# Attention scores of a streaming-encoder layer: the product with the low part of k on 64 rows per map, the two maps in different halves of the array

## The chip, the cores and the metric

One NeuronCore of one Trainium2 chip runs the whole layer as one program. The metric is the time of the program on the device in microseconds (us), as the median of several runs. The profile is one profiled execution on the chip. Its engines are PE (TensorE matmuls), PEld (TensorE weight loads), DVE (VectorE), ACT (ScalarE), POOL (GpSimd) and SP (the queue that issues most DMAs). In a matmul row of a view, `128*96` means 128 rows of the array by 96 columns, and what follows is the shape of the moving operand.

## What is computed

The layer works on 1024 tokens of width 1024: a joint projection, a gated linear recurrence (RG-LRU), differential attention, a cross-attention to 256 memory tokens and a mixture of 32 experts. The change is in the differential attention. It has 8 heads, each with two maps (`m`) of head dimension 64, and a chunk-causal mask:

```python
def diff_attention(q, k, v, ...):
    q = q.reshape(bsz, s, ATTN_HEADS, 2, ATTN_HEAD_DIM)
    k = k.reshape(bsz, s, ATTN_HEADS, 2, ATTN_HEAD_DIM)
    ...
    for blk in range(s // Q_BLOCK):
        q0, q1 = blk * Q_BLOCK, (blk + 1) * Q_BLOCK
        sc = jnp.einsum('bqhmd,bkhmd->bhmqk', q[:, q0:q1], k[:, :q1]).astype(jnp.float32)
        mask = (jnp.arange(q1) // CHUNK)[None, :] <= (jnp.arange(q0, q1) // CHUNK)[:, None]
        p = jax.nn.softmax(jnp.where(mask, sc, NEG_INF), axis=-1)
        w = p[:, :, 0] - lam * p[:, :, 1]
        outs.append(jnp.einsum('bhqk,bkhd->bqhd', w.astype(v.dtype), v[:, :q1]))
```

Everything is float32. The kernel gets its precision by splitting each operand x of a product into two parts, x = high + low, that the array takes as `float32r`.

## The kernel before

**Stages.** q, k and v of all heads are projected first and kept in DRAM. Then comes the attention, head by head, with projections of the gates (`pga`) and of two LRU channels fed in between as filler. After it come the LRU, the merge, the memory attention, the routing and the experts, whose 32 steps stream their weights from DRAM.

**Loading a head.** `head_load(h)` loads q and k of each map twice, to partitions 0 to 63 and to 64 to 127, and splits them. `qS` (per map) has the high part of q in its upper half (partitions 0 to 63) and the low part in its lower half. `kH` (per map) has the high part of k in both halves, and `kL` (per map) has the low part of k in both halves. The tiles come from one pool of 51 slots of 128 x 1024.

**Scores.** `scores(h, qb)` takes a query block of 128 and the nk = qb + 1 key blocks before it. For each map and each piece of keys (`CUTS`: one piece of 256, 384 or 512 keys up to nk = 4, two pieces above) it issues two products into the same PSUM bank: `qS` with `kH` (L474), which gives (high + low) of q times high of k, and `qS` with `kL` (L475), which gives (high + low) of q times low of k. Both use all 128 rows of the array. Up to nk = 4 the two maps lie in two banks of one PSUM tile `pS`; above, each map has a PSUM tile of its own, of two banks. DVE masks (L478, L481) and takes the maximum (L479, L482), ACT takes the exponential (L486). `combine` joins the two maps on POOL and DVE (L495, L496), `w_transpose` turns the result on PE (`pw`, L516) and splits it into `wT` (L519, L520), and `pv` multiplies with v (`po`, lines L152 to L154 of the helper `mm3`).

**Order.** The loop at the end of `filler` calls scores, filler, combine, transposes and products in turn, with the amounts of filler in the table `FV`. A scheduler then settles the order of each engine by a simulated timeline. PE executes its instructions in that order.

Of the kernel before, what the change touches and what calls it, by code (L numbers as in the profile page):

```python
# [20 lines left out]
T = 1024          # tokens  # L21
D = 1024          # model width
P = 128
NB = T // P       # token blocks
NH = 8            # attention heads
NE = 32           # experts
MT = 256          # memory tokens
CAP = 96          # tokens of a block of an expert
# [5 lines left out]
# columns of the packed per-channel vectors  # L34
C_NMIX, C_NMEM = 0, 8
C_CW = 16         # 4 x 8
# [3 lines left out]
# offsets in the packed row vector  # L40
# [4 lines left out]
class Weights:  # L45
    """Streams [128, 1024] float32 weight pieces and splits each exactly into two float32r parts.

    Loads run `load_ahead` pieces before the splits, splits `split_ahead` pieces before their use;
    order-only edges keep the scheduler from running further ahead and taking the slots."""
# [49 lines left out]
    def prefetch(self, n):  # L99
        """Loads up to n pieces ahead of the splits, from the last matmul so far on."""  # L100
        self.floor, self.load_ahead = self.last, n
        self.load()
# [22 lines left out]
def block_kernel(ctx, tc, a):  # L125
# [30 lines left out]
    # ---------------------------------------------------------------- weights  # L156
# [9 lines left out]
    EARLY = [1, 4]      # LRU channels projected beside the attention  # L166
# [26 lines left out]
    # ------------------------------------------------- first loads, constants  # L193
# [23 lines left out]
    def rstd_of(ss, n, cnt, name):  # L217
        """(ss / cnt + eps) ** -0.5 on [128, n]."""
        t = sm.tile([P, 16], F32, tag="rs0", name=name + "m")
        r = sm.tile([P, 16], F32, tag="rs1", name=name + "r")  # L220
        G.tensor_scalar(t[:, :n], ss, 1.0 / cnt, EPS, op0=OP.mult, op1=OP.add)
        G.tensor_tensor(r[:, :n], t[:, :n], negh[:, :n], op=OP.pow)
        return r
# [12 lines left out]
    def transposed(srcs, gain, dst_h, dst_l, name, nk=8):  # L236
        """srcs: token-major tiles; writes [channel, 128 * len(srcs)] per k, scaled by gain[:, k]."""
        n = len(srcs) * P
        for k in range(nk):
            ps = bank(f"{name}p{k}")  # L240
            for j, s in enumerate(srcs):
                E.transpose(ps[:, j * P:(j + 1) * P], s[:, k * P:(k + 1) * P], ident)
            h, l = dst_h(k), dst_l(k)
            A.activation(h, ps[:, :n], AF.Copy, scale=gain[:, k:k + 1])
            V.scalar_tensor_tensor(l, ps[:, :n], gain[:, k:k + 1], f(h), op0=OP.mult, op1=OP.subtract)

    # ------------------------------------------------------ RMSNorm(x), h1^T
# [13 lines left out]
    # -------------------------------------- rotary tables, lambda, q/k gains  # L261
# [52 lines left out]
    # ------------------------- q, k, v: normalised, rotated, kept in DRAM  # L314
    # per head: q, k as [2 maps x 64] x tokens; per head pair: v token-major
# [7 lines left out]
    def tm_proj(w, half, name):  # L323
        """[128 tokens, 4, 256]: the 512 tokens of a half, token-major."""
        ps = bank2(name, F32, (P, 4, 256))
        for j in range(4):
            c = slice((4 * half + j) * P, (4 * half + j) * P + P)
            for k in range(8):
                wh, wl = (x[:, (k % 4) * 256:(k % 4) * 256 + 256] for x in w[k // 4])
                mm3(ps[:, j, :], hH[k][:, c], hL[k][:, c], wh, wl, k == 0, k == 7)  # L330
            if j % 2 == 1:
                W.tick()
            if j == 1:
                yield 5.2
        return ps
# [58 lines left out]
    # ------------------------- merge gates (2 sigmoid - 1 = tanh(x / 2)), in DRAM  # L394
    tg_d = dp.tile([16, P, T], F32, name="tg_d")

    def cm_unit(w, xh, xl, ps_halves):
        """[128 output channels, 1024 tokens], channel-major."""
        wh, wl = w
        for half in range(2):  # L400
            c = slice(half * 512, half * 512 + 512)
            for k in range(8):
                kc = slice(k * P, k * P + P)
                mm3(ps_halves[half], wh[:, kc], wl[:, kc], xh[k][:, c], xl[k][:, c], k == 0, k == 7)
# [22 lines left out]
    # --------------------------------------------------- differential attention  # L427
# [3 lines left out]
    def head_load(h):  # L431
        """Per map: q stacks its two parts on the partitions, k repeats each part."""
# [9 lines left out]
        yield  # L442
        for m in range(2):
            kh_[h, m], kl_[h, m], qs[h, m] = (slot(f"{x}{h}_{m}", F32R) for x in ("kH", "kL", "qS"))
            split(raw.pop((1, m)), kh_[h, m], kl_[h, m])
            yield
            t = raw.pop((0, m))
            A.activation(qs[h, m], t, AF.Copy)
            V.tensor_tensor(qs[h, m][64:128, :], t[64:128, :], f(qs[h, m][64:128, :]), op=OP.subtract)
            del t  # L450
            yield
# [8 lines left out]
    def scores(h, qb):  # L460
# [6 lines left out]
        both = bank2(f"pS{h}_{qb}", F32, (P, 2, 512)) if nk <= 4 else None  # L467
        for m in range(2):
# [3 lines left out]
            lhs = qs[h, m][:, qb * P:(qb + 1) * P]  # L472
            for c in CUTS[nk]:
                E.matmul(ps[:, o:o + c], lhs, kh_[h, m][:, o:o + c], start=True, stop=False)  # L474
                E.matmul(ps[:, o:o + c], lhs, kl_[h, m][:, o:o + c], start=False, stop=True)  # L475
                o += c
            if nk > 4:
                V.memset(ps[0:64, n - 64:n], NEG)  # L478
                V.reduce_max(mx[:, m:m + 1], ps[:, :n], axis=AX.X, negate=True)  # L479
            elif m == 1:  # L480
                V.memset(both[0:64, :, n - 64:n], NEG)  # L481
                V.tensor_reduce(mx, both[:, :, :n], axis=AX.X, op=OP.max, negate=True)  # L482
# [16 lines left out]
    def w_transpose(h, g):  # L499
        """Transposes of the query pair g; parts per two key blocks: [128 keys, 2, 256 queries]."""  # L500
# [121 lines left out]
    for h in range(NH):  # L622
# [12 lines left out]
        for m in range(2):  # L635
            del qs[h, m], kh_[h, m], kl_[h, m]
# [5 lines left out]
    # ------------------------------------------------------------------ RG-LRU  # L642
# [5 lines left out]
    V.tensor_tensor(t1, t0, lam, op=OP.min)                      # -|lam|  # L648
    V.tensor_scalar(t0, t0, 0.0, None, op0=OP.max)
    G.tensor_tensor(t2_, ebase[:, 0:8], t1, op=OP.pow)           # y = exp(-|lam|)  # L650
    V.tensor_scalar(t3, t2_, 2.0, None, op0=OP.add)
    V.reciprocal(t3, t3)
    V.tensor_tensor(t3, t3, t2_, op=OP.mult)                     # z = y / (2 + y)
# [6 lines left out]
    V.scalar_tensor_tensor(t5, t5, 2.0, t0, op0=OP.mult, op1=OP.add)   # softplus(-lam)  # L660
# [48 lines left out]
    def lru_gate(c):  # L709
        """2 * gelu of the gate."""  # L710
# [12 lines left out]
    def lru_scan(c):  # L723
        """Block-diagonal gates, recurrence, times the gate."""
# [25 lines left out]
    # memory keys and values  # L750
# [87 lines left out]
    # --------------------------------- attention output, gated: 2 * sigmoid(g) * y  # L838
# [12 lines left out]
    # -------------------------------------------------- LRU output, merge, w_out  # L851
# [22 lines left out]
    # ------------------------------------------- memory attention, MoE input  # L874
# [20 lines left out]
    def pair_T(src, kp, name):  # L895
        """Channels 256 * kp ... of two token blocks: parts [128 channels, 2 parts, 2, 256 tokens]."""
# [128 lines left out]
    def st_R(tb):  # L1025
        """Transposes of a token block for the router: parts [128 channels, 4, 256 tokens]."""
# [12 lines left out]
    def st_L(g):  # L1039
        """Router logits of two token blocks: [36 high and 36 low parts, 256 tokens]."""  # L1040
# [17 lines left out]
    # ----------------------------------------------------------------- routing  # L1058
    rpool = {}

    def rt(name, *shape, dt=F32):
        """Routing tiles, cut out of slots."""
# [34 lines left out]
    def st_route(b0, n2):  # L1097
        """Choices of n2 token blocks, then their ranks within the experts and dispatch codes."""
# [14 lines left out]
        def first_hot(v, mxv, n):  # L1113
            """One-hot of the first maximum along the last axis."""
# [37 lines left out]
        # weights of the two choices  # L1152
# [12 lines left out]
        # per expert and slot: row code, weight in two parts  # L1165
# [90 lines left out]
    def b3(ap, n):      # [P, NB] -> [P, NB, n]  # L1256
# [11 lines left out]
    def table(code, parts, w_, ix):  # L1268
        """[slots, n]: token - 2 T (0: none), weight parts -> weights, rows (out of bounds: none)."""
# [7 lines left out]
    # ----------------------------------------------------------------- experts  # L1277
# [68 lines left out]
    def more_blocks():  # L1346
        """Blocks beyond the first per expert: count, first and end in the list of such blocks."""
# [42 lines left out]
    # further blocks of experts with more than CAP tokens  # L1390
# [4 lines left out]
    with tc.For_i(0, n_more, 1):  # L1395
# [9 lines left out]
        V.tensor_scalar(eb[:, 2:3], eb[:, 2:3], float(CAP), None, op0=OP.mult)      # -CAP * block of the expert  # L1405
# [40 lines left out]
def _layout(i):  # L1446
# [4 lines left out]
    def cm(m):      # [1024, n * 128] -> [n, 128, 8 * 128]  # L1451
# [3 lines left out]
    def tm(m, c):   # [K, n * c] -> [n, pieces, 128, 1024]  # L1455
# [4 lines left out]
    def col(v):     # [n * 128] -> [128, n]  # L1460
        return v.reshape(-1, 128).T
# [41 lines left out]
```

## Time and profile before

| what | us |
|---|---|
| median of 3 runs | 1963.01 (1957.44 to 1965.14) |
| span of the profiled execution | 1957.1 |
| what lies around the span in the profiled execution | not listed apart; the lowest of the three runs is 0.3 above the span |
| first to last start of a score product (L474, L475) | 328.7 to 720.0 |
| products with `kL` (L475) | 192: 96 of 512 keys, 64 of 256, 32 of 384 |

A view has one row for each group of instructions: line, engine, operation, tiles, shapes, count, busy time and the mean duration of one in ns, and the idle time before it. In a timeline a row has the start, the duration, the instruction, and in brackets how long its engine had been idle and what ended that. Matmuls are pipelined: the next one starts before the record of the last one ends. What a matmul takes of PE is therefore read from start to start.

### The profile page before, as it was taken

To read this page: it belongs to the slowest core of one execution; us is meant where nothing else is said; L and a number is where in the kernel's file an instruction comes from. 1 tells how busy PE (TensorE), PEld (TensorE's weight loads), DVE (VectorE), ACT (ScalarE), POOL (GpSimd) and SP (SyncE) were. 2 spreads that over 40 slices of the span, in tenths; PEclk is the share of its full clock that TensorE was granted. 3 is DMA by queue.
4 is the path that set the end of the run, shared out by engine and by line. 5 is a ranking of instruction groups with operands and counts; after the bars stand their busy time and mean duration, and the time that the engine had idled before them with its cause. 6 is when DMAs were issued, how large, how long until landed. Compare 5 with 4: busy or idle time off the path is not lost. (4 is left out here: it accounts for less than half of the span.)

```text
span 1957.1 us, 27981 instructions
## 1 busy us (share of the span) xinstructions
PE 1882.8 (96%) x10366; PEld 1551.2 (79%) x10366; DVE 1295.3 (66%) x1766; ACT 1087.6 (56%) x1607; POOL 337.1 (17%) x430
## 2 busy tenths in 40 slices
PE   7999999999999999989999999996999999999996
PEld 7999998888888888867888888885777777777664
DVE  5222233777778767887534434776899999999985
ACT  5222223555555545875412214543788888888885
POOL 2343251122222221110000000211111111111110
PEclk9999999999999999989999999998999999999998
DMA  4222225433334322214422511167999999999996
GB/s 167 98 80 94 87 87 152 133 99 115 96 108 120 107 81 79 82 51 173 150 67 84 197 33 65 54 248 296 297 340 361 345 349 360 340 354 342 352 368 217
DMA packets 103130, 353.53 MB, mean 181 GB/s; under 512 B 14224, under 2 KB 15376, under 8 KB 102992
## 3 DMA queue, kind: packets, MB, share of 16 engines
q1 hardware_dynamic: 91088, 322.10, 46.7%
q0 software_dynamic: 7296, 17.04, 3.8%
q10 hardware_dynamic: 4608, 12.58, 1.6%
q8 instruction: 82, 1.34, 0.3%
q14 instruction: 56, 0.46, 0.1%
HBM read 311.82 MB, written 48.23 MB: 184 GB/s over the span
## 5 line engine op out<-in xcount | busy, mean ns | idle before, releaser
L94 DVE TENSOR_TENSOR wl<-wraw,wh 128x1024 fp32r<-128x1024 f32 x480 | 578.4, 1230 | 104.2 <-ACT wh L90 91.9
L90 ACT ACTIVATE wh<-wraw 128x1024 fp32r<-128x1024 f32 x480 | 496.4, 1057 | 111.3 <-DVE wl L94 18.3
L153 PE MATMUL pgu<-wl,xeh 128*96 128x512 f32 x512 | 203.5, 397 | 1.2 <-DVE wl L94 1.0
L152 PE MATMUL pgu<-wh,xeh 128*96 128x512 f32 x512 | 203.4, 397 | 0.3 <-ACT wh L90 0.3
L154 PE MATMUL pgu<-wh,xel 128*96 128x512 f32 x512 | 200.9, 392 | 0.0
L486 ACT ACTIVATE p<-pS,st 128x256 f32<-128x256 f32 (+7 forms) x128 | 94.9, 747 | 93.7 <-DVE st L479 53.2
L154 PE MATMUL pqk<-wh,hL 128*128 128x256 f32 x512 | 145.2, 284 | 0.0
L153 PE MATMUL pqk<-wl,hH 128*128 128x256 f32 x512 | 145.1, 283 | 0.0
L152 PE MATMUL pqk<-wh,hH 128*128 128x256 f32 x512 | 145.0, 283 | 0.0
L152 PE MATMUL pga<-hH,wh 128*128 128x512 f32 x320 | 127.8, 399 | 3.5 <-DVE wT L520 3.5
L153 PE MATMUL pga<-hL,wh 128*128 128x512 f32 x320 | 126.3, 395 | 0.0
L154 PE MATMUL pga<-hH,wl 128*128 128x512 f32 x320 | 125.9, 393 | 0.0
L153 PEld LDWEIGHTS pgu<-wl,xeh 128*96 128x96 f32 x512 | 82.8, 162 | 44.0 <-DVE wl L94 13.0
L152 PEld LDWEIGHTS pgu<-wh,xeh 128*96 128x96 f32 x512 | 82.8, 162 | 33.8 <-ACT wh L90 0.5
L154 PEld LDWEIGHTS pgu<-wh,xel 128*96 128x96 f32 x512 | 82.8, 162 | 33.1 <-DVE xel L321 0.2
L1332 POOL DMA_INDIRECT out<-y,idx x32 | 46.5, 1453 | 357.2 <-ACT y L1331 352.6
L495 POOL TENSOR_SCALAR p<-p,st 128x128 f32<-128x128 f32 (+3 forms) x64 | 55.9, 873 | 294.4 <-DVE st L494 203.4
L153 PE MATMUL py<-wl,ah 128*96 128x512 f32 x256 | 101.8, 398 | 0.5 <-DVE wl L94 0.5
L154 PE MATMUL py<-wh,ah 128*96 128x512 f32 x256 | 100.5, 392 | 0.0
L152 PEld LDWEIGHTS pqk<-wh,hH 128*128 128x128 f32 x512 | 98.2, 192 | 0.0
L153 PEld LDWEIGHTS pqk<-wl,hH 128*128 128x128 f32 x512 | 98.2, 192 | 0.0
L154 PEld LDWEIGHTS pqk<-wh,hL 128*128 128x128 f32 x512 | 98.2, 192 | 0.0
(517 smaller groups left out, 4571.1 us busy)
## 6 DMA issues: line engine op xcount, KB each, us to landing
wraw<-in_w_gu SPq DMA_DIRECT2D x256, 512.0 KB
wraw<-in_w_dn SPq DMA_DIRECT2D x128, 512.0 KB
wraw<-in_w_cm SPq DMA_DIRECT2D x32, 512.0 KB
x<-in_x SPq DMA_DIRECT2D x16, 512.0 KB
wraw<-in_w_qk SPq DMA_DIRECT2D x16, 512.0 KB
qk_d<-qk SPq DMA_DIRECT2D x16, 512.0 KB
qr<-qk_d SPq DMA_DIRECT2D x32, 256.0 KB
kr<-qk_d SPq DMA_DIRECT2D x32, 256.0 KB
```

What stands on the lines that cost most here:

```text
L90: ins = nc.scalar.activation(h, raw, AF.Copy)
L94: nc.vector.tensor_sub(l, raw, h.bitcast(F32))
L152: W.seen(E.matmul(out, lh, rh, start=start, stop=False))
L153: E.matmul(out, lh, rl, start=False, stop=False)
L154: E.matmul(out, ll, rh, start=False, stop=stop)
L486: A.activation(p[:, :n], ps[:, :n], AF.Exp, bias=mx[:, m:m + 1], accum_out=ls[:, m:m + 1])
L495: G.tensor_scalar(pp[1][:, :n], pp[1][:, :n], rl[:, 1:2], 0.0, op0=OP.mult, op1=OP.add)
L1332: G.indirect_dma_start(out=a["out"][:, :], out_offset=bass.IndirectOffsetOnAxis(ap=dest, axis=0), in_=y, in_offset=None, bounds_check=T - ...
```

## The change

`kL` becomes one tile per head. Its upper half holds the low part of k of map 0, and its lower half that of map 1. `qS` of map 1 swaps its halves: low part above, high part below. The product with `kL` takes 64 rows: rows 0 to 63 for map 0 (high part of q), rows 64 to 127 for map 1 (high part of q). The low part of q times the low part of k is no longer computed. The products with `kL` of both maps are written behind those with `kH` of both maps, in turn map 0, map 1. The line of the `kH` product is now L479, that of the `kL` product L485.

```diff
+        kl_[h] = slot(f"kL{h}", F32R)
         for m in range(2):
-            kh_[h, m], kl_[h, m], qs[h, m] = (slot(f"{x}{h}_{m}", F32R) for x in ("kH", "kL", "qS"))
-            split(raw.pop((1, m)), kh_[h, m], kl_[h, m])
+            kh_[h, m], qs[h, m] = (slot(f"{x}{h}_{m}", F32R) for x in ("kH", "qS"))
+            own, other = ((slice(0, 64), slice(64, 128)), (slice(64, 128), slice(0, 64)))[m]
+            t = raw.pop((1, m))
+            A.activation(kh_[h, m], t, AF.Copy)
+            V.tensor_tensor(kl_[h][own, :], t[own, :], f(kh_[h, m][own, :]), op=OP.subtract)
             yield
             t = raw.pop((0, m))
             A.activation(qs[h, m], t, AF.Copy)
-            V.tensor_tensor(qs[h, m][64:128, :], t[64:128, :], f(qs[h, m][64:128, :]), op=OP.subtract)
+            V.tensor_tensor(qs[h, m][other, :], t[other, :], f(qs[h, m][other, :]), op=OP.subtract)
...
+        qc = slice(qb * P, (qb + 1) * P)
         for m in range(2):
...
-            lhs = qs[h, m][:, qb * P:(qb + 1) * P]
             for c in CUTS[nk]:
-                E.matmul(ps[:, o:o + c], lhs, kh_[h, m][:, o:o + c], start=True, stop=False)
-                E.matmul(ps[:, o:o + c], lhs, kl_[h, m][:, o:o + c], start=False, stop=True)
+                E.matmul(ps[:, o:o + c], qs[h, m][:, qc], kh_[h, m][:, o:o + c], start=True, stop=False)
                 o += c
+        o = 0
+        for c in CUTS[nk]:
+            for m in range(2):
+                r = slice(64 * m, 64 * m + 64)
+                E.matmul(pss[m][:, o:o + c], qs[h, m][r, qc], kl_[h][r, o:o + c], start=False, stop=True)
+            o += c
+        for m in range(2):
+            ps = pss[m]
             if nk > 4:
                 V.memset(ps[0:64, n - 64:n], NEG)
```

The rest of the diff takes out comments and moves line numbers. Two places show what becomes of the order on PE.

The first is PE at head 0, query block 3 (nk = 4, one piece of 512 keys), before the change. `kH_0`, `qS_0` are the tiles of map 0, `kH_1`, `qS_1` those of map 1, and `pga` is filler:

```order
L152 MATMUL pga_1_3526<-hH_148,wh_3173 128x512
L474 MATMUL pS_3_3545<-kH_0_3349,qS_0_3351 128x512
L475 MATMUL pS_3_3545<-kL_0_3350,qS_0_3351 128x512
L474 MATMUL pS_3_3545<-kH_1_3356,qS_1_3358 128x512
L475 MATMUL pS_3_3545<-kL_1_3357,qS_1_3358 128x512
L153 MATMUL pga_1_3526<-hL_156,wh_3173 128x512
```

The same place after the change:

```order
L152 MATMUL pga_1_3525<-hH_148,wh_3173 128x512
L479 MATMUL pS_3_3544<-kH_0_3350,qS_0_3351 128x512
L479 MATMUL pS_3_3544<-kH_1_3356,qS_1_3357 128x512
L485 MATMUL pS_3_3544<-kL_3349,qS_0_3351 128x512
L485 MATMUL pS_3_3544<-kL_3349,qS_1_3357 128x512
L153 MATMUL pga_1_3525<-hL_156,wh_3173 128x512
```

The two products with `kL` now stand next to each other, map 0 in the upper half, map 1 in the lower.

The second place is PE at head 0, query block 4 (nk = 5, pieces of 512 and 256 keys, a PSUM tile for each map), before the change:

```order
L474 MATMUL pS_4_0_3592<-kH_0_3349,qS_0_3351 128x512
L475 MATMUL pS_4_0_3592<-kL_0_3350,qS_0_3351 128x512
L474 MATMUL pS_4_0_3592<-kH_0_3349,qS_0_3351 128x256
L475 MATMUL pS_4_0_3592<-kL_0_3350,qS_0_3351 128x256
L153 MATMUL pga_0_3569<-hL_155,wh_3404 128x512
L154 MATMUL pga_0_3569<-hH_147,wl_3405 128x512
```

The same place after the change; the four rows of map 1 follow directly behind the last row shown:

```order
L479 MATMUL pS_4_0_3591<-kH_0_3350,qS_0_3351 128x512
L479 MATMUL pS_4_0_3591<-kH_0_3350,qS_0_3351 128x256
L485 MATMUL pS_4_0_3591<-kL_3349,qS_0_3351 128x512
L485 MATMUL pS_4_0_3591<-kL_3349,qS_0_3351 128x256
L153 MATMUL pga_0_3568<-hL_155,wh_3403 128x512
L154 MATMUL pga_0_3568<-hH_147,wl_3404 128x512
L152 MATMUL pga_0_3568<-hH_148,wh_3403 128x512
L153 MATMUL pga_0_3568<-hL_156,wh_3403 128x512
L154 MATMUL pga_0_3568<-hH_148,wl_3404 128x512
L152 MATMUL po_0_3609<-wT_0_0_3514,vH_3362 128x256
L153 MATMUL po_0_3609<-wT_0_0_3514,vH_3362 128x256
L154 MATMUL po_0_3609<-wT_0_0_3514,vL_3363 128x256
```

Here the scheduler keeps the maps apart, as it did before: all of map 0, then other work, then all of map 1. Counted over the whole order, the 192 products with `kL` stand in 96 groups without any other matmul inside. In 33 places a product of one map stands directly before the same piece of the other map (16 pieces of 256 keys, 8 of 384, 9 of 512); the other 126 stand beside products of their own half, or alone. The order of DVE, ACT, POOL and SP changes in a handful of places by one to four rows.

More of the change, by code (lines that the diff above doesn't have):

```diff
@@ L635, in block_kernel @@
         for m in range(2):
-            del qs[h, m], kh_[h, m], kl_[h, m]
+            del qs[h, m], kh_[h, m]
+        del kl_[h]
     while later:
```

## The prediction

> **What bounds the kernel now.** I first read the head of the page, then the busy time of the engines by stretches of the span, then the waits of PE inside the attention.
>
> ```profile
> span 1957.1 us, 27981 instructions
> PE 1882.8 (96%) x10366; PEld 1551.2 (79%) x10366; DVE 1295.3 (66%) x1766; ACT 1087.6 (56%) x1607; POOL 337.1 (17%) x430
> ```
>
> ```profile
> core 0: us, PE busy (x) PEld busy (x) DVE busy (x) ACT busy (x) POOL busy (x), PEclk, DMA share, GB/s
> 328.00:722.00 394.00, 381.52 (x2146) 328.05 (x2145) 290.24 (x570) 224.41 (x484) 86.36 (x153) 1.00 0.36 107
> 722.00:1340.00 618.00, 601.15 (x2883) 499.53 (x2882) 371.33 (x482) 275.88 (x411) 51.79 (x73) 0.99 0.33 116
> 1370.00:1957.00 587.00, 569.38 (x2688) 399.32 (x2688) 516.03 (x521) 482.44 (x572) 79.08 (x63) 0.99 0.96 335
> ```
>
> The reader is to see that PE is the engine without slack. In the attention (328 to 722 us) it is busy 381.5 of 394 us, while DVE has 290 and ACT 224, and DMA is at a third. The granted clock is full. What a matmul there takes more or less of PE therefore moves all that follows. The later stages can give nothing back: PE is at 97% in both rows below.
>
> ```profile
> engine line waited for: us in total, times, longest us
> PE pS L474 <- ACT p L486: 7.7, 11, 2.5
> PE pga L152 <- DVE wT L520: 3.5, 4, 1.0
> PE pw L516 <- DVE p L496: 0.5, 1, 0.5
> ```
>
> All that PE waits for others in the attention is 11.7 us. Most of it is the score product waiting for its PSUM tile, which the exponential still reads. These 11.7 us are also the most that a longer PE stream could take back, and it would be only a part, since the exponentials move later with the scores. I count a change of PE time in full.
>
> **What the products cost.** The groups of the `kL` product by shape:
>
> ```profile
> L475 PE MATMUL pS<-kL,qS 128*128 128x512 f32 x96 | 37.7, 393 | 0.0
> L475 PE MATMUL pS<-kL,qS 128*128 128x256 f32 x64 | 17.7, 284 | 0.0
> L475 PE MATMUL pS<-kL,qS 128*128 128x384 f32 x32 | 11.1, 346 | 0.0
> ```
>
> The means are durations of pipelined records, so the price is read from start to start in the timeline:
>
> ```profile
> 602.61 0.39 PE L474 MATMUL pS<-kH,qS 128*128 128x512 f32 x1
> 602.83 0.39 PE L475 MATMUL pS<-kL,qS 128*128 128x512 f32 x1
> 603.06 0.28 PE L474 MATMUL pS<-kH,qS 128*128 128x256 f32 x1
> 603.17 0.28 PE L475 MATMUL pS<-kL,qS 128*128 128x256 f32 x1
> 603.29 0.40 PE L152 MATMUL pga<-hH,wh 128*128 128x512 f32 x1
> ...
> 439.63 0.34 PE L475 MATMUL pS<-kL,qS 128*128 128x384 f32 x1
> 439.81 0.34 PE L474 MATMUL pS<-kH,qS 128*128 128x384 f32 x1
> 439.98 0.33 PE L475 MATMUL pS<-kL,qS 128*128 128x384 f32 x1
> 440.15 0.28 PE L152 MATMUL po<-wT,vH 128*128 128x256 f32 x1
> ```
>
> A product of 512 keys takes 0.225 us (602.61 to 602.83 to 603.06), one of 256 takes 0.115 (603.06 to 603.17 to 603.29), one of 384 takes 0.173 (439.63 to 440.15 in three steps). All of the `kL` products together are 96 x 0.225 + 64 x 0.115 + 32 x 0.173 = 34.5 us of PE.
>
> **What the change can save.** Where two products in different halves of the array stand next to each other and run at the same time, one of the two is saved. That is possible in the 33 places of the new order: 16 x 0.115 + 8 x 0.173 + 9 x 0.225 = **5.3 us**, no more. If all 192 stood in pairs it would be half of 34.5, some 17 us, but from five key blocks on, where most of the keys are, the order keeps the maps apart: a `kL` product has one of its own half or a 128-row product on both sides. A single 64-row product still streams the same number of keys, so I give it the same time; no row of this profile has one of 64 rows.
>
> **What the change adds.** In the order before, nothing ever uses less than the whole height of the array as a part of its own. Now PE goes 96 times from products over the whole array to products in a half and 96 times back: **192 switches**. What a switch costs is not shown before the change, so I bound it.
>
> From below, the nearest row is a change in the number of rows, when the transposes of the expert stage use 96 rows between products of 128:
>
> ```profile
> 1496.53 0.39 PE L154 MATMUL pgu<-wh,xel 128*96 128x512 f32 x1
> 1496.76 0.82 PE L1292 MATMUL pxe<-ident,xe 96*128 96x96 f32 x8
> 1497.37 0.45 PE L152 MATMUL pgu<-wh,xeh 128*96 128x512 f32 x1
> 1497.66 0.39 PE L153 MATMUL pgu<-wl,xeh 128*96 128x512 f32 x1
> ...
> L1292 PE MATMUL pxe<-ident,xe 96*128 96x96 f32 x256 | 27.1, 250 | 7.0 <-DMA xe<-h_d,idx 7.0
> ```
>
> The eight transposes take 0.82 us from the first start to the last end, one lasts 0.25, so they follow each other every 0.57 / 7 = 0.081 us. Eight of them and one product of 512 are 8 x 0.081 + 0.225 = 0.87 us, and from 1496.76 to 1497.66 there are 0.90. Two changes of the number of rows thus cost 0.03 us: **0.01 to 0.02 us each**, as good as nothing. A cost below nothing is left out for the switch itself, since nothing becomes shorter by it; what the halves gain is the 5.3 us above.
>
> From above there are two things that a switch could uncover. One is the weight load. As a rule it lies under the product before; where it could not start early, the timeline shows its price, first in the rows of PE, then in those of the weight loads of the same place:
>
> ```profile
> 576.67 0.50 PE L474 MATMUL pS<-kH,qS 128*128 128x512 f32 x1 [1.12 <-ACT p L486]
> 577.01 0.39 PE L475 MATMUL pS<-kL,qS 128*128 128x512 f32 x1
> ...
> 577.70 0.47 PE L474 MATMUL pS<-kH,qS 128*128 128x512 f32 x1
> 578.01 0.40 PE L475 MATMUL pS<-kL,qS 128*128 128x512 f32 x1
> 578.24 0.39 PE L474 MATMUL pS<-kH,qS 128*128 128x512 f32 x1
> ```
>
> ```profile
> 577.01 0.19 PEld L474 LDWEIGHTS pS<-kH,qS 128*128 128x128 f32 x1
> ...
> 577.67 0.19 PEld L474 LDWEIGHTS pS<-kH,qS 128*128 128x128 f32 x1 [0.24 <-ACT p L486]
> ```
>
> After an idle PE (576.67) the product takes 0.34 us to the next start in place of 0.225: an uncovered weight load is **0.11 us**. At 577.70 its load came only 0.03 before it, and it took 0.31, so 0.08 was uncovered. The other thing is the end of a product that has to leave the array and reach PSUM before the next may start: a record lasts 0.39 and the next starts after 0.225, so the rest is **0.165 us**. Both one after the other are 0.275 us, the upper end. Between the ends 0 and 0.275 I take 0.11: it is the row nearest to a switch among those where PE loses anything at all, a weight load that could not go ahead of the product before. The sum: 192 x 0.11 - 5.3 = 21.1 - 5.3 = **+15.8 us**.
>
> The Trainium skill, page "TensorEngine Tiling (Array Packing)", section "Tiling Modes", speaks against this change: going over to another tiling, not only to another tile of the same tiling, empties the TensorE. No run here shows it; by it the sum would be +26.4 us if only the rest of a product is waited for, and +47.5 us with the weight load behind it (worked out below). The page "TensorE: Matmul & The Clock Gate", section "Part 3: Packing small matmuls", says that matmuls in different row groups start about 4 ns apart, an estimate by which the 33 pairs would give their 5.3 us in full.
>
> **What else changes.** DVE writes the low part of k on 64 partitions in place of 128:
>
> ```profile
> L449 DVE TENSOR_TENSOR qS<-qr,qS x16: 1222/1223/1612, 323.7 to 677.7; 64x1024 fp32r<-64x1024 f32 x16
> L321 DVE TENSOR_TENSOR kL<-kr,kH x16: 1197/1219/1428, 322.4 to 667.8; 128x1024 fp32r<-128x1024 f32 x16
> ```
>
> The same operation takes 1.22 us at 64 and at 128 partitions, so DVE saves nothing; it has 104 us free in the attention anyway. One slot of 51 is freed per head. PE waits in the attention for PSUM and for transposed tiles (the three rows above), never for a tile from that pool, so I give it nothing; if it let weights load earlier, DMA at 0.36 has room and nobody waits. The score tile of up to four key blocks is ready when its last product is, as before; above that each map still comes whole, so masks and maxima wait no longer than before. The moved `kL` products add no wait: they read tiles of a head that were split before its first score product, as now.
>
> **Against the runs.** Per the profiled execution, span 1957.1 + 15.8 = 1972.9 us. The median of the runs is 5.9 above that span, and the runs spread over 7.7 us; carried over, 1963.0 + 15.8 = **1979 us**. About 0.5% (9.8 us) is what a measurement of this kernel can tell from no change.
>
> **The rivals.**
> *The switch is free* (the other side: not slower). As with 96 rows, PE would step over it, at 0.02 us or less. Then the sum is at best -5.3 us, 1957.7, and without any overlap of the halves 0 to +4 us, to 1967. The point that decides is a switch of 5.3 / 192 = 0.028 us for faster or slower at all, and (5.3 + 9.8) / 192 = 0.079 us for slower by over 0.5%. For it: the 96-row rows above. Against it: those transposes still use the array as one piece.
> *A full emptying at each switch*: the rest of the product and then the weight load, 0.275 us. 192 x 0.275 - 5.3 = +47.5 us, 2010.5. For it speaks that the rows of before never show a half, so nothing excludes it; against it that PE otherwise starts a weight load as soon as the product before has begun (both rows at 577.01: the load of the next product starts with the product). The rule of the page "TensorEngine Tiling (Array Packing)" in the Trainium skill is this rival. With the rest of the product alone, 192 x 0.165 - 5.3 = +26.4 us, 1989.4, which I count with the forecast.
> *The halves never overlap*: the forecast without its credit, +21.1 us, 1984. It lies inside the forecast's range.
>
> **How the numbers follow.** One thing uncovered at each switch, 0.08 to 0.165 us, 1973 to 1990, has 0.45. The free switch, 1957.7 to 1967, has 0.32. More than that, up to the full emptying and a little beyond, 1990 to 2016, has 0.20. Something outside these (a shift in the order that helps, the freed slot) has 0.03 for faster by over 0.5%. Of the forecast's 0.45 I leave 0.04 for a switch just under 0.079 us, which would count as the same. So faster 0.03, same 0.36, slower 0.61. The range takes in the free switch at its best, with 1.7 us for the spread of the runs, and the full emptying with its price of 0.275: 1956 to 2012; beyond it stay some 0.1.
>
> **What would show it.** In the new profile the start after a `kH` product and before the first `kL` product of a group shows one side of the switch, and the start from the last `kL` product to the next 128-row one the other: 0.225 us plus the price for 512 keys. The two `kL` products of a pair start almost together if the halves overlap, and 0.225 apart if they don't. The last score product starts at 720 us plus most of the change; PE stays at 97% of the attention. The prediction is wrong if those steps are the same 0.225 as before, or if PE idles for something else, for example `pS` waiting longer for ACT.

## The result and the profile after

| | before | after |
|---|---|---|
| median of 4 runs | 1964.08 us (1957.44 to 1968.34) | 1986.06 us (1984.46 to 1988.78) |
| span of the profiled execution | 1957.1 us | 1982.7 us |

The ratio is 1.012, with a 95% interval of 1.0102 to 1.0139: some 22 us slower, where +15.8 was forecast. The spans differ by 25.6 us. The four runs of before spread over 10.9 us and lie high: in the three series of the experiments, with 9 to 23 runs of the same kernel each, its median is 1960.8 to 1962.1 us, and against those the change is 24 to 25 us slower.

The head of the page after the change, the busy time by stretches (engines as before the change; each stretch moved by what the attention grew), and the waits of PE inside the attention:

```profile
span 1982.7 us, 27998 instructions
PE 1912.7 (96%) x10366; PEld 1544.1 (78%) x10366; DVE 1294.8 (65%) x1766; ACT 1088.9 (55%) x1607; POOL 335.5 (17%) x430
```

```profile
328.00:745.00 417.00, 410.73 (x2138) 319.78 (x2137) 288.56 (x568) 224.57 (x483) 84.74 (x153) 0.99 0.34 101
745.00:1363.00 618.00, 600.05 (x2879) 498.84 (x2879) 372.56 (x483) 275.57 (x409) 51.92 (x73) 0.99 0.33 115
1395.00:1982.00 587.00, 569.68 (x2689) 400.02 (x2688) 516.02 (x521) 482.85 (x573) 78.58 (x63) 0.99 0.96 336
```

```profile
PE pS L479 <- ACT p L498: 3.9, 3, 2.3
PE pga L152 <- DVE wT L532: 1.7, 3, 0.7
PE pw L528 <- DVE p L508: 0.5, 1, 0.5
```

The stretch of the attention is 417 us in place of 394, and PE is busier in it, not idler. The two long stretches behind it take as long as before, 618 and 587 us, with nearly the same busy times. The last score product starts 24.1 us later, so nearly all of the 25.6 us is lost in the attention. The other 1.5 us lie behind it and are less than the runs differ there without a change: from the start of the last score product to the end there are 1237.1 us before, 1238.6 after, 1239.4 in e1 and 1241.6 in e5 (both below). PE waits less for the others, 6.1 us in place of 11.7.

Where it goes is seen in the timeline of PE and of the weight loads at a query block whose maps stand apart. The row at 619.78 holds the two products of one map with `kL`, of 512 and 256 keys, now with 64 rows:

```profile
619.11 0.39 PE L154 MATMUL pga<-hH,wl 128*128 128x512 f32 x1
619.35 0.50 PE L479 MATMUL pS<-kH,qS 128*128 128x512 f32 x2
619.78 0.62 PE L485 MATMUL pS<-kL,qS 64*128 64x512 f32 x2
620.33 0.50 PE L152 MATMUL pga<-hH,wh 128*128 128x512 f32 x1
620.66 0.39 PE L153 MATMUL pga<-hL,wh 128*128 128x512 f32 x1
620.89 0.40 PE L154 MATMUL pga<-hH,wl 128*128 128x512 f32 x1
```

```profile
619.12 0.42 PEld L479 LDWEIGHTS pS<-kH,qS 128*128 128x128 f32 x2
619.77 0.29 PEld L485 LDWEIGHTS pS<-kL,qS 64*128 64x128 f32 x2 [0.24 <-issue]
620.32 0.19 PEld L152 LDWEIGHTS pga<-hH,wh 128*128 128x128 f32 x1 [0.25 <-issue]
620.43 0.19 PEld L153 LDWEIGHTS pga<-hL,wh 128*128 128x128 f32 x1
```

A product of 512 and one of 256 keys take 0.34 us of PE together. From the `kH` products to the `kL` products there are 0.43 (619.35 to 619.78): **0.09 us** too much. The weight load of `kL`, which else starts with the product before, starts only at 619.77, together with its own product. So it is uncovered: from 619.78 to 620.33 there are 0.55, that is about 0.34 for the two products, **0.11** for the load, and 0.09 again at the way back. The first product back, at 620.33, again starts with its load and takes 0.33 in place of 0.225. A switch thus costs both: some 0.09 in which neither the next product nor its load starts, and 0.11 for the load that did not start ahead. The Trainium skill, page "TensorEngine Tiling (Array Packing)", section "Tiling Modes", says that going to another tiling empties the TensorE; the trace fits that, with 0.09 us before the load and the load on top of it. That the 0.09 is the emptying itself is not shown.

Where the two maps stand as a pair, they do share the array:

```profile
611.08 0.63 PE L479 MATMUL pS<-kH,qS 128*128 128x512 f32 x2
611.64 0.50 PE L485 MATMUL pS<-kL,qS 64*128 64x512 f32 x2
612.07 0.50 PE L152 MATMUL pga<-hH,wh 128*128 128x512 f32 x1
```

From 611.64 to 612.07 there are 0.43 us for two products of 512 keys: 0.225 + 0.20, so the second one takes no time of its own.

### The profile page after: what moved, and what is told of

It reads as the page before. It is cut to its first block, busy times and chain, and to the rows that moved or that the text cites. A ratio compares the mean times of both kernels' runs of the same rounds, so it can differ in the third digit from the quotient of the medians.

```text
span 1982.7 us, 27998 instructions
## 1 busy us (share of the span) xinstructions
PE 1912.7 (96%) x10366; PEld 1544.1 (78%) x10366; DVE 1294.8 (65%) x1766; ACT 1088.9 (55%) x1607; POOL 335.5 (17%) x430
```

## The experiments

The theory after the result (A): each switch costs 0.20 us of PE, each pair saves one product, and waits for other engines take part of it back. Rivals: only the weight load of 0.11 is uncovered (B); the new order costs the time, not the switches (C); it is the use of fewer rows, not the cutting of the array.

**e1: the new order on the whole array.** The kernel before, with only its order changed:

```diff
             for c in CUTS[nk]:
                 E.matmul(ps[:, o:o + c], lhs, kh_[h, m][:, o:o + c], start=True, stop=False)
-                E.matmul(ps[:, o:o + c], lhs, kl_[h, m][:, o:o + c], start=False, stop=True)
                 o += c
+        o = 0
+        for c in CUTS[nk]:
+            for m in range(2):
+                E.matmul(pss[m][:, o:o + c], qs[h, m][:, qb * P:(qb + 1) * P], kl_[h, m][:, o:o + c], start=False, stop=True)
+            o += c
...
```

> The kernel before, with its low-part products on all 128 rows, but written in the order of the change: both maps with kH first, then both maps with kL, in the same 96 groups. If the switches between the whole array and a half cost the time (A), nothing is left: within 4 us of the kernel before. If the new order costs it, because the scores of the first map wait for those of the second (C), the loss of some 22 us stays.

Measured: 1962.19 against 1961.77 us, ratio 1.0008 (0.9995 to 1.002). In the attention its trace has the same 2132 matmuls in the same order as that of the change. The order costs nothing; C falls.

**e2: the same half for both maps.** As e1, with `[0:64, ...]` on the rows of both operands of the low-part product.

> As e1, but the low-part products use rows 0 to 63 for both maps, so the 96 groups and 192 switches of the change stand, and no two products can share the array. The low part of q times the low part of k is left out, as in the change. If the two halves of the changed kernel overlap, its 33 pairs save 5.2 us there, and this one is about 5 us slower than the changed kernel: +25 to +31 us on the kernel before. If the overlap was worth nothing, it equals the changed kernel, +22 us.

Measured: 1987.37 against 1961.77, ratio 1.014 (1.0124 to 1.0155), +25.6 us by the medians. The interval meets that of the change, so the totals alone don't settle what the overlap saves. The timeline of PE does, at a place like the pair above:

```profile
612.68 0.73 PE L479 MATMUL pS<-kL,qS 64*128 64x512 f32 x2
613.34 0.50 PE L152 MATMUL pga<-hH,wh 128*128 128x512 f32 x1
```

Two products of 512 keys in one half take 0.66 us, against 0.43 in two halves: one product of 0.225 is saved by the overlap. e2 has the same order of matmuls too, so the starts of all three can be compared one by one: around 95 of the 96 groups (the last one ends the stretch) PE takes 33.5 us more than e1 here and 28.5 after the change. The overlap is worth 5.0 us of PE. Of these 2.3 arrive in the time: from the first to the last score product the attention takes 418.2 us here and 415.9 after the change.

**e3: all products in pairs.** The changed kernel with an order-only edge, after which 64 groups hold all 96 pairs:

```diff
-                E.matmul(ps[:, o:o + c], qs[h, m][:, qc], kh_[h, m][:, o:o + c], start=True, stop=False)
+                lastH = E.matmul(ps[:, o:o + c], qs[h, m][:, qc], kh_[h, m][:, o:o + c], start=True, stop=False)
...
-                E.matmul(pss[m][:, o:o + c], qs[h, m][r, qc], kl_[h][r, o:o + c], start=False, stop=True)
+                W.after(E.matmul(pss[m][:, o:o + c], qs[h, m][r, qc], kl_[h][r, o:o + c], start=False, stop=True), lastH)
```

> The changed kernel with an order-only edge from the last kH product of a query block to its kL products: 64 groups in place of 96, and all 192 kL products in 96 pairs, which save 17.2 us. A (tail of the product before, 0.09, and the weight load, 0.11, at each of 128 switches): 25.6 - 17.2 = +8 us on the kernel before. B (the weight load alone, 0.11): 14.1 - 17.2 = -3 us.

Measured: 1991.48 against 1961.77, ratio 1.0155 (1.0141 to 1.0169), +30 us. Both A and B missed. The waits of PE in the attention show a second cost:

```profile
PE pS L479 <- ACT p L498: 16.1, 17, 2.3
PE pw L528 <- DVE p L508: 5.3, 7, 1.3
PE pw L528 <- DVE wT L532: 2.0, 4, 1.0
```

PE now waits for the exponential to free the score tiles 17 times, 16.1 us, and for `combine` 5.3 us; before it was 7.7 and 0.5. Whether that is the edge or the halves was left to e8.

**e4: each `kL` product behind its `kH` product.** The changed kernel with the two calls in one loop, as the kernel before has them: 384 switches.

> The changed kernel with each kL product right behind its kH product, as the kernel before has them: 192 groups of one product, 384 switches, no pair. A (0.20 us a switch): 76.8 us more of PE, less what PE waits less for others, of which there are 12 us before: +62 to +77 us. B (0.11 us a switch): +42 us at most.

Measured: 2030.13 against 1961.77, ratio 1.034 (1.0318 to 1.0363), +68 us by the medians: within A's 62 to 77, far from B's 42. The timeline of PE at a block of eight key blocks, where whole array and half alternate:

```profile
618.73 0.50 PE L480 MATMUL pS<-kH,qS 128*128 128x512 f32 x1 [0.80 <-ACT p L494]
619.16 0.49 PE L481 MATMUL pS<-kL,qS 64*128 64x512 f32 x1
619.58 0.50 PE L480 MATMUL pS<-kH,qS 128*128 128x512 f32 x1
620.01 0.49 PE L481 MATMUL pS<-kL,qS 64*128 64x512 f32 x1
620.43 0.50 PE L480 MATMUL pS<-kH,qS 128*128 128x512 f32 x1
620.87 0.50 PE L481 MATMUL pS<-kL,qS 64*128 64x512 f32 x1
621.29 0.49 PE L480 MATMUL pS<-kH,qS 128*128 128x512 f32 x1
621.72 0.50 PE L481 MATMUL pS<-kL,qS 64*128 64x512 f32 x1
```

Seven steps take 2.99 us, 0.427 each, where a product takes 0.225: a switch costs 0.20 us, the same into the half and out of it. This kernel has the order of the kernel before; compared start by start, the steps around all 384 switches grew by 69.8 us, 0.18 each. So 0.20 is the price between long products, and the mean is a little lower.

**e5: 96 rows, not cut.** As e1, with `[0:96, ...]` on the rows of both operands of the low-part product.

> The order of e1, with the low-part products on rows 0 to 95, so that the array is still used as one piece. Of the low part of q times the low part of k, half of the channels are left out. If what costs is that fewer than 128 rows are used, the loss of the change comes back (+22 us or so). If what costs is cutting the array in two, nothing: within 4 us of the kernel before.

Measured: 1962.49 against 1960.75, ratio 1.001 (0.9998 to 1.0022). Its timeline of PE:

```profile
609.26 0.51 PE L474 MATMUL pS<-kH,qS 128*128 128x512 f32 x2
609.61 0.52 PE L479 MATMUL pS<-kL,qS 96*128 96x512 f32 x2
609.96 0.40 PE L154 MATMUL pga<-hH,wl 128*128 128x512 f32 x1
```

A group of 512 and 256 keys takes 0.35 us with 128 and with 96 rows, 0.01 above the two products. So it is not the smaller number of rows as such: 96 rows are free, and 64 rows cost 0.20 us a switch, also in e2, where nothing runs in the other half. That the array is cut in two at 64 rows and stays whole at 96 is the reading that fits both; no view shows the cut itself.

**e6 and e7: one part of the change alone.** `kL` is kept whole for each map, and the rows depend on the block:

```diff
-                r = slice(64 * m, 64 * m + 64)
+                r = slice(64 * m, 64 * m + 64) if nk <= 4 else slice(0, 128)
```

e7 has `nk > 4` in its place.

> The change for query blocks with up to four key blocks alone: 33 groups in halves, 31 of them pairs. The rest is on the whole array, in the same order. Low part of q times low part of k is left out for these blocks. By A, 0.40 us of PE a group: 33 x 0.40 - 4.9 saved by the pairs = +8 us of PE, of which waits take some back, +4 to +8 us. If only long runs of the array matter, 0 or below.

> The change for query blocks with more than four key blocks alone: 63 groups in halves, 2 pairs in them. Low part of q times low part of k is left out for these blocks. By A: 63 x 0.40 - 0.3 = +25 us of PE, +16 to +25 us in time. Together with e6 the loss of the change, +22 to +25 us, should come out.

Measured: e6 1965.17 against 1960.75, ratio 1.0024 (1.0013 to 1.0034), +4.4 us; e7 1979.11, ratio 1.0097 (1.0077 to 1.0117), +18.4 us. Together 22.8 us, close to the 22.0 of the change. Where nearly every group is a pair, the pairs give back over a third of the switches' 13 us; where the scheduler keeps the maps apart, next to nothing.

**e8: the order of e3 on the whole array.** e1 with the edge of e3.

> The order of e3 with the same edge, on the whole array: no half, no switch, no pair that saves. If the 18 us or so by which e3 is slower than its switches and pairs come to is the price of the edge (the scores of the first map wait for those of the second, and PE waits for PSUM), this kernel is +13 to +18 us on the kernel before. If the halves themselves cost it, this one is within 4 us of the kernel before.

Measured: 1979.43 against 1962.05, ratio 1.0093 (1.0074 to 1.0111), +17.4 us, with the same kinds of waits of PE:

```profile
PE pS L474 <- ACT p L492: 17.6, 20, 2.6
PE pw L522 <- DVE p L502: 3.5, 4, 1.3
PE pw L522 <- DVE wT L526: 3.5, 5, 1.0
```

The edge itself costs 17 us. That it does so because the first map's scores wait for the second map's PSUM tile fits the 17.6 us on `pS`, but was not tried apart. What the halves add in this order is e3 less e8, 29.7 - 17.4 = 12.3 us by the medians, and 1989.3 - 1980.8 = 8.5 us between the two profiled executions, of which 420.3 - 414.5 = 5.8 us lie from the first to the last score product. A's 25.6 - 17.2 = 8.4 lies among these. The built orders of the two are not the same product for product, so the difference is no closer test. In the timeline of e3 a group with two pairs shows its two switches and no further cost:

```profile
627.35 0.51 PE L479 MATMUL pS<-kH,qS 128*128 128x512 f32 x2
627.79 0.62 PE L485 MATMUL pS<-kL,qS 64*128 64x512 f32 x4
628.34 0.39 PE L154 MATMUL po<-wT,vL 128*128 128x256 f32 x1
628.56 0.39 PE L153 MATMUL pga<-hL,wh 128*128 128x512 f32 x1
```

The four `kL` products, two of 512 and two of 256 keys, take 0.55 us, that is 0.34 for the two pairs and 0.20 as in the group of the changed kernel above.

No version beat the kernel before. A group between long products costs two switches, 0.40 us, so it has to save two products of 512 keys, 0.45, to gain anything; only the largest query block reaches that, and only with all of its pairs in one group.

## Why the prediction was right

**What bounds the kernel: right.** PE time in the attention sets the end. The last score product starts at 744.1 us in place of 720.0, and the later stretches kept their lengths. DVE's subtraction brought nothing: DVE is busy 288.6 us in the attention, before 290.2. The freed slot shows no gain, but was not tried apart.

**What the change saves: right.** The 33 pairs start together, and counted over all starts of the trace they save 5.2 us of PE (5.3 in the prediction).

**What a switch costs: the mechanism was half of it, and its size too small.** The step was to take 0.11 between the ends 0 and 0.275, the weight load alone. Measured were 0.20: the load of 0.11 and a wait of 0.09 in front of it. The rival of a full emptying had the mechanism right, both one after the other, and its price too high: it took 0.165 for the first part from the length of a record, of which only 0.09 is lost. So 0.20 lies above the 0.08 to 0.165 us that the forecast gave a switch, and below the full emptying. 96 groups x 0.40 - 5.2 = 33.2 us of PE, in place of 15.8.

**Counting PE time in full: wrong, and it hid part of that error.** From the first to the last score product the attention grew by 24.6 us (391.3 to 415.9), not 33.2. The starts of the change against those of e1, in the same order, show where the rest went. Around the same 95 groups PE lost 28.5 us: of these, 41 in front of a product of 512 columns cost 0.385 us each (median), 19 in front of one of 128 columns 0.34, and 5 that lie beside a wait of PE for another engine 0.6 together. Elsewhere PE takes some 4 us less, where its waits for other engines are shorter by 5. In e4, where 384 switches are 76.8 us at 0.20, the attention grew by 66.4. The prediction had looked at the 11.7 us that PE waited before as the most that could come back, and then took none of it. That the forecast came as near as +15.8 to the +22 is therefore luck in part: a switch priced too low and waits that were not taken back err in opposite directions. At 0.20 us a switch and PE time in full the forecast would have been +33.

**The sign and the range** came from the count in the order, 192 switches against 33 pairs, and e6 and e7 show that count at work.

## What to carry to other kernels

Count the switches between the whole array and parts of it before counting what the parts save: here each switch cost 0.20 us of PE, nearly as much as a product of 512 columns. Put as many products in parts as possible behind each other, and look in the built order whether they stand in pairs, since a scheduler that sees two tiles may keep them apart. An edge that forces the pairs can cost as much in waits as the pairs save (17.4 against 17.2 us here): test it with the edge alone.

## What the runs showed of the hardware

That two 64-row products in different halves start together was expected (3 ns apart in the trace); that their weight loads do, too, was not: the two loads of the pair are over after 0.19 us in the view of the loads, and after 0.29 where both products lie in the same half (619.77 above):

```profile
611.64 0.19 PEld L485 LDWEIGHTS pS<-kL,qS 64*128 64x128 f32 x2 [0.36 <-issue]
```

And the number of rows and the tiling are two things: going from 128 to 96 rows and back cost 0.01 us for a group, going to 64 rows cost 0.40.
